# An encoder trunk on one core: the first norm's scale and shift made tile by tile, and one instruction order kept out of 24

## The chip, the cores and the metric

The kernel runs on one core of one Trainium2 chip. The core has a matrix engine (TensorE, PE in the profile), a vector engine (VectorE, DVE), a scalar engine (ScalarE, ACT), a general engine (GpSimd, POOL), and a sync engine (SyncE, SP) from whose queue this kernel issues its DMAs. Sixteen DMA engines move data between the memory of the chip and the core. The metric is the time of one execution on the device in microseconds, median of several runs; less is better.

## The reference, cut to what matters

One layer over 2048 tokens of 1024 features, all in float32: a norm whose scale and shift come from a conditioning vector, a combined projection, three kinds of recurrent heads, an output projection, a second such norm and a gated feed-forward block.

```python
cond = silu(c)                                   # (1, 1024)
mod = cond @ ada_w + ada_b                       # (1, 6 * 1024)
sh_m, sc_m, g_m, sh_f, sc_f, g_f = split(mod, 6)
h = rms_norm(x, norm_mix) * (1.0 + sc_m) + sh_m  # the first norm and its modulation
proj = h @ w_in
...                                              # retention, RWKV-7, mLSTM on parts of proj
x = x + g_m * (mixed @ w_out)
h = rms_norm(x, norm_ffn) * (1.0 + sc_f) + sh_f
gate, up = split(h @ ffn_w_in, 2)
x = x + g_f * ((silu(gate) * up) @ ffn_w_out)
return rms_norm(x, final_norm)
```

The change touches how `sh_m` (1024 shifts, 1024 x 1024 weights) and `sc_m` (as many) are made, and when.

## The kernel before

Everything is held transposed: features on the 128 partitions, tokens along the free dimension. The 1024 features are 8 tiles of 128 (`KT = 8`), the 2048 tokens are 4 blocks of 512 (`T`). A projection column (128 outputs of `w_in`, a "slot" of `winA`) is 8 weight tiles of 128x128, one for each feature tile, and each is multiplied three times (`mm3`: high weight with high data, high with low, low with high part) so that float32 precision comes out of fp32r passes; that makes 24 matmuls of 128x512 a column and block. Before use a weight half (256 KB) is loaded into a buffer `wraw`, cast to its high part by ScalarE (`split_in`) and subtracted to its low part by VectorE or GpSimd.

**Order.** The program text does not issue anything directly. Each call (`tt`, `stt`, `act`, `mmi`, `dma` ...) is recorded by `Sched.wrap` with its engine, an estimate of its cost and the tiles that it reads and writes. `Sched.emit` then lays all of them out with a list scheduler: each engine takes, among the operations that are ready by the estimates, the one of the best priority of its stage (`PRIO`) and then of the lowest place in the program. A result counts as ready for another engine after a latency from a table plus `margin`, 0.16 us. Dependences go by whole tiles. The operations are issued in that order, so each engine's order is fixed at build time, and every instruction has the one line L343 in the profile, that of the issuing loop. Buffers of a kind (`tag`) are given out in the order of first use.

**Lanes.** `dense()` does the projections and the feed-forward block (stages A, U, G, F), lanes P, C and M the recurrent heads, `ada_late()` the later modulation vectors, and `warm()` records 18 dummy matmuls at the lowest priority, which fill holes at the start.

**The head of `dense()`**, which the change rewrites, deals with block 0:

- Four tiles of `ada0` (the 1024 columns of `ada_w` that make `sh_m`, 128 rows each, 512 KB) are loaded into buffers `big`, then the 8 tiles of x (`xload`, 256 KB each), then the conditioning vector to all partitions (`cond_load`, tile `cond`, 512 KB), then the other four `ada0` tiles.
- `ada_shift`: TensorE multiplies the column `csil[:, k]` with each `ada0` tile, in two halves of 512 outputs, summed over all 8 tiles in PSUM (tile `dn`). ScalarE copies the two rows out, 8 tiny matmuls turn them into columns and one VectorE operation adds the bias: `shift_m`, all 8 tiles' shifts at once.
- `Sumsq` squares the x tiles (ScalarE), adds them up (VectorE, tile `acc`), and `fin` turns the sum into 1/rms, spread over all partitions (`bc`, in the tile `acc`): transposes on TensorE, a reduction on VectorE, a power on GpSimd (`rrs`), matmuls and a copy.
- `ada(1, m, ...)` makes the scale of feature tile m on VectorE: it loads 512 KB of `adaT`, the transposed `ada_w`, into one of 4 buffers `g` (tile `adaw`), multiplies with `cond` and sums along the row (accumulated output) into `gain_m[m]`.
- The first projection loop runs over feature tiles m = 0 to 7: the scale is finished, x is multiplied by `bc`, ScalarE and VectorE make the high and low part `h` (buffers `big`), and the 3 matmuls of each column loaded so far follow; five columns in all (two in `w`, three in spare tiles AR/ATA, ATB/BKt, UV/mt). So the loop holds 5 x 8 x 3 = 120 matmuls of 128x512.

There are 9 buffers `big`: `cond`, and the 8 `ada0` tiles, which give way to the 8 tiles `h`. The shifts and scales serve the later blocks too (`gsh_m`).

Of the kernel before, what the change touches and what calls it, by code (L numbers as in the profile page):

```python
# [50 lines left out]
for _n, _w in CONST_SPEC:  # L51
# [7 lines left out]
CFG = dict(w=4, raw=4, big=9, g=4, x=8, tmp=5, per=2, vd=1, nt=2, inv=1, xi=1, pr=1, x2=1, ld=2, wg=2, t1=4, gb=4, base=1, mt=2, mc=8,  # L59
           cv=1, mb=1, r1=4, dn=4, mx=2, ch=1, ml=1, bc=2, s2=1, hold=2.5, margin=0.16, warm=18, ahead=2, sm=1, a1=2, wm=0, wc=0.4, fa=True, ff=True, fh=True, nw=5, ws=2, fp=(0, 3, 6))  # L60
PRIO = dict(W=99, U=-20, A=-8, G=2, F=3, C=-7.5, P=-5, M=-4.9, S=-4)
# [3 lines left out]
class Sched:  # L65
# [9 lines left out]
    def __init__(self, prio, margin):  # L75
        self.ops = []
        self.stage = ("A", 0)
        self.prio = prio
        self.margin = margin
        self.flags = set()  # L80
        self.hist = {}
        self.bufs = {}
        self.psum = set()
        self.changes = 0

# [96 lines left out]
    def emit(self):  # L182
        import heapq

        n = len(self.ops)
# [22 lines left out]

        tag_of, uses, queue, free = {}, {}, {}, {}
        for tag, h in self.hist.items():  # L210
            h = sorted((x for x in h if x in touch), key=lambda x: touch[x][0])
            queue[tag] = h[::-1]
            free[tag] = [0.0] * self.bufs[tag]
            for x in h:
                tag_of[x] = tag
                uses[x] = len(set(touch[x]))
                left[touch[x][0]] += 1
        ready = [0.0] * n
        time = {e: 0.0 for e in self.ENG}
# [39 lines left out]
        while True:  # L259
# [56 lines left out]
            if e == "pe":  # L316
                m = op[2][e][2]
                if m != pe_mode:
                    end += 0.2 if op[2][e][0] > 0.1 and m == whole else 0.095
                    pe_mode = m  # L320
                    self.changes += 1
            chosen[j] = e
            time[e] = end
            order.append((t, j))
            for i in succ[j]:
                e2 = self.ops[i][0]
                r = end + self.LAT[e][e2]
                if e != e2:
                    r += self.margin
                met(i, r)  # L330
# [7 lines left out]
        assert len(order) == n, "a cycle through the buffers"  # L338
        self.end = max(time.values())
        order.sort()  # L340
        for t, j in order:
            op = self.ops[j]
            op[2][chosen[j]][1](*op[5], **op[6])  # L343


@with_exitstack
def trunk(ctx: ExitStack, tc: tile.TileContext, a: dict):
# [57 lines left out]
    def dps():  # L405
        return L.tile(pd, [P, 512], F32, "dn", K["dn"], nm("dn"))
# [10 lines left out]
    def tmp():  # L417
        return L.tile(tp, [P, 512], F32, "tmp", K["tmp"], nm("tmp"))
# [89 lines left out]
    gain_m = [cp.tile([P, 1], F32, name=f"gain_m{k}") for k in range(KT)]  # L508
    shift_m = cp.tile([P, KT], F32, name="shift_m")
    gbias = cp.tile([P, KT], F32, name="gbias")  # L510
# [3 lines left out]
    def gsh_m(k):  # L514
        return gain_m[k], shift_m[:, k:k + 1]
# [1265 lines left out]
def _prep(inp):  # L1781
# [30 lines left out]
    def put(name, v):  # L1812
# [47 lines left out]
```

## Time and profile before

| what | value |
|---|---|
| median of 3 runs | 2838.6 us (2829.53 to 2845.41) |
| the profiled execution | 2837.28 us |
| its span in the profile | 2835.5 us |
| mean granted TensorE clock | 0.994 of full |
| TensorE busy | 2763.7 us, 97% of the span |
| VectorE busy | 1927.6 us, 68% |

The profiled execution is 1.8 us longer than its span, and 1.3 us under the median. Times in the profile count from the start of the span. A matmul's busy time overlaps that of the next, so its rate is read from the starts of successive ones. "Idle before" names what an engine waited for last.

### The profile page before, as it was taken

To read this page: it belongs to the slowest core of one execution; us is meant where nothing else is said; L and a number is where in the kernel's file an instruction comes from. 1 tells how busy PE (TensorE), PEld (TensorE's weight loads), DVE (VectorE), ACT (ScalarE), POOL (GpSimd) and SP (SyncE) were. 2 spreads that over 40 slices of the span, in tenths; PEclk is the share of its full clock that TensorE was granted. 3 is DMA by queue.
4 is the path that set the end of the run, shared out by engine and by line. 5 is a ranking of instruction groups with operands and counts; after the bars stand their busy time and mean duration, and the time that the engine had idled before them with its cause. 6 is when DMAs were issued, how large, how long until landed. Compare 5 with 4: busy or idle time off the path is not lost.

```text
span 2835.5 us, 43320 instructions
## 1 busy us (share of the span) xinstructions
PE 2763.7 (97%) x14378; PEld 2263.1 (80%) x14378; DVE 1927.6 (68%) x5505; ACT 841.9 (30%) x1793; POOL 888.7 (31%) x1082
## 2 busy tenths in 40 slices
PE   8999999999999999999999999999999999999998
PEld 5877877887787787888778787787778888788887
DVE  6788789787787978764788877658778763422223
ACT  4445335434434433333322221122131211200002
POOL 2325645534536364431434132222223300000001
PEclk9999999999999999999999999999999999999999
DMA  8976556456655678888886556577765557775553
GB/s 321 318 229 196 158 170 195 144 163 230 203 154 157 226 237 262 280 281 306 263 279 195 185 184 199 183 246 241 237 196 171 181 194 241 258 248 192 194 193 137
DMA packets 349806, 613.04 MB, mean 216 GB/s; under 512 B 95528, under 2 KB 172944, under 8 KB 349584
## 3 DMA queue, kind: packets, MB, share of 16 engines
q1 hardware_dynamic: 349584, 610.29, 66.0%
q8 instruction: 114, 1.87, 0.3%
q14 instruction: 108, 0.88, 0.1%
HBM read 471.42 MB, written 138.73 MB: 215 GB/s over the span
## 4 chain that ended last, share of the span: by engine, by line
PE 74%; DVE 13%; DMA 7%; issue 2%; ACT 1%; POOL 1%; SPq 1%; POOLq 0%; DVEq 0%; ACTq 0%
PE dn L343 63%; PE mx L343 5%; PE ml L343 3%; PE ch L343 3%; DVE pr L343 2%; DVE tmp L343 2%; DMA tmp<-in_xT 1%; DVE mc L343 1%; DVE t L343 1%; DVE xi L343 1%; DMA w<-wsave 1%; DVE x L343 1%; SPq L343 1%; DMA adaw<-in_adaT 1%; DMA out<-x 1%
## 5 line engine op out<-in xcount | busy, mean ns | idle before, releaser
L343 PE MATMUL dn<-h,w 128*128 128x512 f32 x6648 | 1640.1, 398 | 13.0 <-DVE h L343 6.1
L343 PEld LDWEIGHTS dn<-h,w 128*128 128x128 f32 x6648 | 1223.1, 189 | 258.4 <-DVE h L343 10.7
L343 PE MATMUL dn<-g,w 128*128 128x512 f32 (+1 forms) x2112 | 506.8, 392 | 7.5 <-DMA w<-wsave 3.7
L343 PEld LDWEIGHTS dn<-g,w 128*128 128x128 f32 x2112 | 382.1, 188 | 84.6 <-issue 3.0
L343 POOL TENSOR_TENSOR w<-wraw,w 128x512 fp32r<-128x512 f32 (+1 forms) x243 | 315.0, 1298 | 395.1 <-ACT w L343 307.2
L343 ACT CAST w<-wraw 128x512 fp32r<-128x512 f32 (+1 forms) x414 | 246.1, 595 | 511.2 <-PE dn L343 357.5
L343 DVE TENSOR_TENSOR pr<-base,xi 128x20 f32<-128x20 f32 (+23 forms) x768 | 245.6, 320 | 26.4 <-POOL xi L343 12.4
L343 DVE SCALAR_TENSOR_TENSOR tmp<-tmp,dn 128x512 f32<-128x512 f32 x96 | 65.7, 685 | 250.5 <-PE dn L343 249.9
L343 DVE SCALAR_TENSOR_TENSOR x<-dn,mod,x 128x512 f32<-128x512 f32 x192 | 141.6, 747 | 118.9 <-PE dn L343 115.5
L343 PE MATMUL dn<-mT,w 128*128 128x512 f32 x768 | 187.6, 396 | 1.4 <-DMA w<-wsave 1.3
L343 DVE TENSOR_TENSOR w<-wraw,w 128x512 fp32r<-128x512 f32 (+1 forms) x171 | 114.8, 674 | 79.4 <-ACT w L343 74.9
L343 PEld LDWEIGHTS dn<-mT,w 128*128 128x128 f32 x768 | 141.3, 188 | 31.1 <-DMA w<-wsave 2.5
L343 POOL TENSOR_TENSOR rrs<-rst,mhalf 128x4 f32<-128x4 f32 (+1 forms) x13 | 15.6, 1203 | 465.2 <-DVE rst L343 443.7
L343 ACT ACTIVATE tmp<-dn 128x512 f32<-128x512 f32 x108 | 64.3, 596 | 313.1 <-PE dn L343 312.6
L343 DVE TENSOR_REDUCE xi<-pr 128x16 f32<-128x256 f32 (+30 forms) x768 | 146.3, 190 | 11.3
L343 ACT CAST g<-tmp 128x512 fp32r<-128x512 f32 x88 | 54.6, 620 | 309.3 <-DVE tmp L343 309.0
L343 PE MATMUL dn<-w,h 128*128 128x324 f32 x768 | 128.6, 319 | 2.3 <-DVE w L343 1.6
L343 PEld LDWEIGHTS dn<-w,h 128*128 128x128 f32 x768 | 116.1, 190 | 3.9 <-DVE w L343 1.8
L343 DVE SCALAR_TENSOR_TENSOR mc<-cv,pcol,mc 96x256 f32<-96x256 f32 x192 | 108.7, 566 | 11.6 <-ACT mc L343 9.8
L343 POOL TENSOR_SCALAR rSd<-rS,dfac 128x128 f32<-128x128 f32 x93 | 65.9, 709 | 147.3 <-DVE rS L343 111.6
L343 ACT COPY Y<-ch 64x128 f32<-64x128 f32 x93 | 24.1, 259 | 174.0 <-PE ch L343 172.5
L343 DVE SCALAR_TENSOR_TENSOR rS<-ch,dfac,rSd 64x64 f32<-64x64 f32 x186 | 52.4, 282 | 31.8 <-PE ch L343 27.5
(301 smaller groups left out, 3331.3 us busy)
## 6 DMA issues: line engine op xcount, KB each, us to landing
w<-wsave SPq DMA_DIRECT2D x440, 512.0 KB, 3.6
wsave<-w SPq DMA_DIRECT2D x148, 512.0 KB, 4.2
wraw<-in_winA SPq DMA_DIRECT2D x208, 256.0 KB, 3.1
wraw<-in_wfi SPq DMA_DIRECT2D x88, 256.0 KB, 3.6
adaw<-in_adaT SPq DMA_DIRECT2D x40, 512.0 KB, 5.9
tmp<-in_xT SPq DMA_DIRECT2D x72, 256.0 KB, 4.0
base<-nbuf SPq DMA_DIRECT2D x24, 512.0 KB, 5.6
wraw<-in_wfo SPq DMA_DIRECT2D x44, 256.0 KB, 5.3
```

The source lines that it names most:

```text
L343: op[2][chosen[j]][1](*op[5], **op[6])
```

## The change

The modulation of feature tile m becomes a step of its own, `modulation(m)`, made just ahead of that tile's turn in the loop; `ada_shift` goes away. For m = 1, 3, 5, 7 the 128 shifts come from TensorE (`shift_pe`): one 512 KB block of `ada0`, which the host lays out anew so that it holds all 1024 rows for the 128 columns of tile m, and 8 matmuls that use the 128x128 pieces as weights and one column of `csil` as data, into the PSUM buffer of lane C (`cps`); VectorE adds the bias out of PSUM. For m = 0, 2, 4, 6 they come from VectorE (`shift_dve`), as the scales do, from `adaT`. The shifts stand in two tiles, even and odd. The weights of the TensorE shifts use buffers `big`, together with `cond` and the 8 tiles `h`; those of VectorE the 4 buffers `g`. The squares of x come ahead of `cond` in the program.

`emit` now lays the whole program out 24 times, with margins of 0.160, 0.162, ... 0.206 us, and issues the order whose last engine ends first by the scheduler's own estimates. That concerns the order of all 43,000 instructions, not the head alone.

```diff
-CFG = dict(..., hold=2.5, margin=0.16, warm=18, ...)
+CFG = dict(..., hold=2.5, margin=0.16, layouts=24, mstep=0.002, warm=18, ...)
+PE_SHIFT = (1, 3, 5, 7)
...
+        best = None
+        for i in range(CFG["layouts"]):
+            r = self.layout(self.margin + CFG["mstep"] * i, succ, list(left), touch, tag_of, dict(total), firsts)
+            if best is None or r[0] < best[0]:
+                best = r
+        self.end, order, chosen = best
+        for t, j in order:
+            op = self.ops[j]
+            op[2][chosen[j]][1](*op[5], **op[6])
+
+    def layout(self, margin, succ, left, touch, tag_of, uses, firsts):
...
-    shift_m = cp.tile([P, KT], F32, name="shift_m")
+    shifts = [cp.tile([P, KT // 2], F32, name=f"shift_m{k}") for k in range(2)]
+    shift_m = [shifts[k % 2][:, k // 2:k // 2 + 1] for k in range(KT)]
...
-    def ada0_load(k):
-        w = L.tile(bp, [P, D], F32, "big", K["big"], nm("adaw"))
-        dma(w, a["ada0"][k * P:(k + 1) * P, :])
-        return w
-
-    def ada_shift(ws):
-
-        pss = [dps(), dps()]
-        for k, w in enumerate(ws):
-            yield [mmi(pss[i][0:1, :], csil[:, k:k + 1], w[:, i * 512:(i + 1) * 512], k == 0, k == KT - 1) for i in range(2)]
-        row = tmp(), tmp()
-        for r, ps in zip(row, pss):
-            acopy(r[0:1, :], ps[0:1, :])
-        pcol_ = dps()
-        yield [mmi(pcol_[:, k:k + 1], row[k // 4][0:1, (k % 4) * P:(k % 4 + 1) * P], ones[0:1, 0:1], True, True)
-               for k in range(KT)]
-        tt(shift_m, pcol_[:, 0:KT], pcs("ada_b", 0, KT), ALU.add)
+    def shift_pe(m):
+
+        w = L.tile(bp, [P, D], F32, "big", K["big"], nm("adaw"))
+        dma(w, a["ada0"][m])
+        ps = cps()
+        yield [mmi(ps[:, 0:1], w[:, k * P:(k + 1) * P], csil[:, k:k + 1], k == 0, k == KT - 1) for k in range(KT)]
+        tt(shift_m[m], ps[:, 0:1], pcs("ada_b", m), ALU.add)
+
+    def shift_dve(m):
+        ada(0, m, gp, "g", K["g"], shift_m[m])
+        tt(shift_m[m], shift_m[m], pcs("ada_b", m), ALU.add)
+
+    def gain_dve(m):
+        ada(1, m, gp, "g", K["g"], gain_m[m])
+        stt(gain_m[m], gain_m[m], gbias[:, m:m + 1], pcs("norm_mix", m), ALU.add, ALU.mult)
...
-        aw = [ada0_load(k) for k in range(4)]
         x0 = [xload(0, k) for k in range(KT)]
-        cond_load()
-        aw += [ada0_load(k) for k in range(4, KT)]
-        yield from ada_shift(aw)
         for k in range(KT):
             q.add(x0[k], True)
-
-        def ada_first(m):
-            ada(1, m, gp, "g", K["g"], gain_m[m])
-
-        for m in range(K["a1"]):
-            ada_first(m)
+        cond_load()
+
+        def modulation(m):
+            if m in PE_SHIFT:
+                yield from shift_pe(m)
+            else:
+                shift_dve(m)
+            gain_dve(m)
+
+        yield from modulation(0)
...
         for m in range(KT):
-            if m >= K["a1"]:
-                ada_first(m)
+            if m:
+                yield from modulation(m)
...
-            stt(g, g, gbias[:, m:m + 1], pcs("norm_mix", m), ALU.add, ALU.mult)
...
-"ada0": np.ascontiguousarray(f("ada_w")[0][:, 0:D]),
+"ada0": np.ascontiguousarray(f("ada_w")[0][:, 0:D].reshape(KT, P, KT, P).transpose(2, 1, 0, 3)).reshape(KT, P, D),
```

## Rows read from the trace of the kernel before

**Rows 1.** The page, part 1: busy us and share of each engine.

```profile
PE 2763.7 (97%) x14378; PEld 2263.1 (80%) x14378; DVE 1927.6 (68%) x5505; ACT 841.9 (30%) x1793; POOL 888.7 (31%) x1082
```

**Rows 2.** Windows: busy us (instructions) by engine, clock, DMA share, GB/s.

```profile
10.00:20.00 10.00, 7.02 (x34) 3.43 (x33) 3.92 (x6) 4.97 (x9) 0.41 (x1) 0.99 1.01 376
20.00:30.00 10.00, 10.00 (x29) 2.75 (x27) 5.31 (x11) 2.53 (x5) 2.04 (x2) 0.84 1.00 388
30.00:40.00 10.00, 4.82 (x22) 3.85 (x23) 9.94 (x14) 7.09 (x13) 5.29 (x3) 0.67 0.73 254
40.00:50.00 10.00, 10.00 (x37) 8.00 (x37) 8.83 (x17) 5.38 (x10) 1.03 (x1) 0.81 0.99 324
...
60.00:70.00 10.00, 10.00 (x46) 8.23 (x45) 6.57 (x14) 3.97 (x7) 3.62 (x3) 1.00 0.97 352
```

**Rows 3.** Timeline of 0 to 45 us: start, length, instruction, idle before.

```profile
6.61 7.03 PE L343 MATMUL dn<-adaw,csil 128*1 128x512 f32 x16 [0.54 <-DMA adaw<-in_ada]
...
18.18 0.63 ACT L343 ACTIVATE tmp<-cond 128x512 f32<-128x512 f32 x1 [2.72 <-DMA cond<-in_c]
...
24.71 0.66 PE L343 MATMUL dn<-const,acc 128*128 128x128 f32 x4
...
29.41 0.61 ACT L343 CAST w<-wraw 128x512 fp32r<-128x512 f32 x1
...
29.91 1.94 PE L343 MATMUL dn<-const,tmp 1*128 1x1 f32 x16
30.02 0.58 ACT L343 COPY acc<-dn 128x512 f32<-128x512 f32 x1
...
30.66 0.74 DVE L343 SCALAR_TENSOR_TENSOR x<-x,gain_m,acc 128x512 f32<-128x512 f32 x1
...
35.29 0.16 DVE L343 TENSOR_TENSOR shift_m<-dn,pcol 128x8 f32<-128x8 f32 x1
...
36.26 0.79 PE L343 MATMUL dn<-h,w 128*128 128x512 f32 x1 [4.41 <-ACT h L343]
...
37.82 2.50 PE L343 MATMUL dn<-h,w 128*128 128x512 f32 x5 [0.77 <-DVE h L343]
...
40.12 1.05 PE L343 MATMUL dn<-h,AR 128*128 128x512 f32 x2
```

**Rows 4.** Timeline of 45 to 90 us: the end of the first projection loop.

```profile
64.42 1.53 PE L343 MATMUL dn<-h,w 128*128 128x512 f32 x6
...
65.79 0.62 PE L343 MATMUL dn<-h,AR 128*128 128x512 f32 x2
...
67.84 18.98 PE L343 MATMUL dn<-h,w 128*128 128x512 f32 x83
```

**Rows 5.** Lines, VectorE, 30 to 68 us: count, busy us, mean ns, idle.

```profile
L343 DVE SCALAR_TENSOR_TENSOR adaw<-adaw,cond 128x1024 f32<-128x1024 f32 x10 | 13.1, 1320 | 0.0
L343 DVE TENSOR_TENSOR x<-x,acc 128x512 f32<-128x512 f32 x7 | 5.6, 797 | 0.0
L343 DVE TENSOR_TENSOR h<-x,h 128x512 fp32r<-128x512 f32 x7 | 5.3, 775 | 0.4 <-ACT x L343 0.4
L343 DVE SCALAR_TENSOR_TENSOR gain_m<-gain_m,gbias,pcol 128x1 f32<-128x1 f32 x7 | 4.2, 594 | 0.0
...
L343 DVE TENSOR_TENSOR ATA<-wraw,AR 128x512 fp32r<-128x512 f32 x2 | 1.4, 679 | 0.0
```

**Rows 6.** Windows of 2 us, 36:38 to 44:46: the clock, behind POOL.

```profile
36.00:38.00 2.00, 0.97 (x2) 0.47 (x3) 2.00 (x4) 1.97 (x4) 0.49 (x1) 0.50 0.72 272
...
42.00:44.00 2.00, 2.00 (x7) 1.57 (x6) 2.00 (x4) 0.00 (x0) 0.00 (x0) 0.57 1.02 341
44.00:46.00 2.00, 2.00 (x11) 1.61 (x10) 1.22 (x4) 1.61 (x3) 0.00 (x0) 1.00 0.95 318
```

**Rows 7.** Windows: 100 us to the end, columns as in the second group.

```profile
100.00:2835.00 2735.00, 2676.62 (x14023) 2201.87 (x14021) 1860.17 (x5386) 794.57 (x1713) 854.25 (x1043) 1.00 0.65 213
```

**Rows 8.** Waits of TensorE, 100 us to the end: total, times, longest.

```profile
PE dn L343 <- DMA w<-wsave: 7.2, 8, 1.8
```

More of the change, by code (lines that the diff above doesn't have):

```diff
@@ L59 @@
 CFG = dict(w=4, raw=4, big=9, g=4, x=8, tmp=5, per=2, vd=1, nt=2, inv=1, xi=1, pr=1, x2=1, ld=2, wg=2, t1=4, gb=4, base=1, mt=2, mc=8,
-           cv=1, mb=1, r1=4, dn=4, mx=2, ch=1, ml=1, bc=2, s2=1, hold=2.5, margin=0.16, warm=18, ahead=2, sm=1, a1=2, wm=0, wc=0.4, fa=True, ff=True, fh=True, nw=5, ws=2, fp=(0, 3, 6))
+           cv=1, mb=1, r1=4, dn=4, mx=2, ch=1, ml=1, bc=2, s2=1, hold=2.5, margin=0.16, layouts=24, mstep=0.002, warm=18, ahead=2, sm=1, a1=2, wm=0, wc=0.4, fa=True, ff=True, fh=True, nw=5, ws=2, fp=(0, 3, 6))
 PRIO = dict(W=99, U=-20, A=-8, G=2, F=3, C=-7.5, P=-5, M=-4.9, S=-4)
@@ L83, in __init__ @@
         self.psum = set()
-        self.changes = 0
     def tile(self, pool, shape, dt, tag, bufs, name):
@@ L182, in emit @@
     def emit(self):
-        import heapq
         n = len(self.ops)
@@ L207, in emit @@
                 touch.setdefault(x, []).append(j)
-        tag_of, uses, queue, free = {}, {}, {}, {}
+        tag_of, total, firsts = {}, {}, {}
         for tag, h in self.hist.items():
             h = sorted((x for x in h if x in touch), key=lambda x: touch[x][0])
-            queue[tag] = h[::-1]
-            free[tag] = [0.0] * self.bufs[tag]
+            firsts[tag] = h[::-1]
             for x in h:
                 tag_of[x] = tag
-                uses[x] = len(set(touch[x]))
+                total[x] = len(set(touch[x]))
                 left[touch[x][0]] += 1
+        best = None
[8 more added lines that the diff above has]
+    def layout(self, margin, succ, left, touch, tag_of, uses, firsts):
+        import heapq
+        n = len(self.ops)
+        queue = {tag: list(h) for tag, h in firsts.items()}
+        free = {tag: [0.0] * self.bufs[tag] for tag in firsts}
         ready = [0.0] * n
@@ L320, in emit @@
                     pe_mode = m
-                    self.changes += 1
             chosen[j] = e
@@ L328, in emit @@
                 if e != e2:
-                    r += self.margin
+                    r += margin
                 met(i, r)
@@ L338, in emit @@
         assert len(order) == n, "a cycle through the buffers"
-        self.end = max(time.values())
         order.sort()
-        for t, j in order:
-            op = self.ops[j]
-            op[2][chosen[j]][1](*op[5], **op[6])
+        return max(time.values()), order, chosen
 @with_exitstack
@@ L514, in gsh_m @@
     def gsh_m(k):
-        return gain_m[k], shift_m[:, k:k + 1]
-    def ada0_load(k):
+        return gain_m[k], shift_m[k]
+    def shift_pe(m):
         w = L.tile(bp, [P, D], F32, "big", K["big"], nm("adaw"))
-        dma(w, a["ada0"][k * P:(k + 1) * P, :])
-        return w
-    def ada_shift(ws):
-        pss = [dps(), dps()]
-        for k, w in enumerate(ws):
-            yield [mmi(pss[i][0:1, :], csil[:, k:k + 1], w[:, i * 512:(i + 1) * 512], k == 0, k == KT - 1) for i in range(2)]
-        row = tmp(), tmp()
-        for r, ps in zip(row, pss):
-            acopy(r[0:1, :], ps[0:1, :])
-        pcol_ = dps()
-        yield [mmi(pcol_[:, k:k + 1], row[k // 4][0:1, (k % 4) * P:(k % 4 + 1) * P], ones[0:1, 0:1], True, True)
-               for k in range(KT)]
-        tt(shift_m, pcol_[:, 0:KT], pcs("ada_b", 0, KT), ALU.add)
+        dma(w, a["ada0"][m])
[8 more added lines that the diff above has]
+        stt(gain_m[m], gain_m[m], gbias[:, m:m + 1], pcs("norm_mix", m), ALU.add, ALU.mult)
     def ada_late():
@@ L1835, in _prep @@
         "xT": np.ascontiguousarray(x.T), "c": f("c"),
-        "adaT": np.ascontiguousarray(f("ada_w")[0].T), "ada0": np.ascontiguousarray(f("ada_w")[0][:, 0:D]),
+        "adaT": np.ascontiguousarray(f("ada_w")[0].T), "ada0": np.ascontiguousarray(f("ada_w")[0][:, 0:D].reshape(KT, P, KT, P).transpose(2, 1, 0, 3)).reshape(KT, P, D),
         "ccol": np.ascontiguousarray(f("c").reshape(KT, P).T),
```

## The prediction

> **What bounds the kernel now.** I read the page's busy shares first: TensorE is busy 97% of the span [rows 1]. From 100 us to the end it stands idle 58.4 us of 2735, at full clock [rows 7], and the largest group of waits in that stretch is 7.2 us in eight pieces, the longest 1.8 us [rows 8]. So from 100 us on the kernel is a queue of TensorE work with small holes; what can be gained there in one place is small, and work that TensorE starts earlier should bring the end forward by about as much.
>
> Next the windows of the first 70 us [rows 2] and the timeline behind them [rows 3]. From 10 to 30 us the DMA engines are full (share 1.01 and 1.00, 376 and 388 GB/s), while TensorE does only the shifts, dummies and the norm's small matmuls. The first matmul of the projection loop starts at 36.26 us, after a wait of 4.41 us for ScalarE's `h`; `h` waited for the shifts, whose last step ran at 35.29. The loop's last matmul is issued just before 67.84, and 83 more follow without a hole [rows 4]. So 36.26 to 67.84 us, 31.6 us for 120 matmuls, is TensorE's own time. At full clock they follow one another at 0.228 us (six from 64.42 to 65.79 [rows 4]), 27.4 us; the other 4.2 us are mostly the lower clock: the granted clock is 0.50, the 1.2 GHz level, from 36 us and full from 44 [rows 6], and five matmuls from 37.82 take until 40.12 [rows 3], 0.46 us each, twice the full rate.
>
> The head is thus bound by loads, then by a chain through the shifts, and from 36 us by TensorE, with VectorE nearly as full (9.94 of 10 us in 30 to 40, 8.83 in 40 to 50 [rows 2]).
>
> **Part 1: the start of the loop.** Before the first `h`, eight 512 KB tiles of `ada0` have to land. Afterwards it is one 512 KB tile of `adaT`. At 382 GB/s, the mean of the two full windows [rows 2], such a tile takes 1.37 us.
>
> - `cond`: ScalarE got it at 18.18 us after waiting for that load [rows 3]. Four `ada0` loads go from ahead of it, 5.5 us: 12.7 us. The x tiles are ahead of it in the queue, the last in by about 11.3.
> - The norm: from the transposes of the squares' sum at 24.71 us to the end of the copy of `bc` at 30.60 is 5.9 us [rows 3]. The transposes stood behind the shifts' matmuls, which go. With a square and an add after the last x (1.4 us) they start near 12.7, and `bc` is ready at 18.6.
> - Tile 0's shift and scale: two `adaT` loads behind `cond` land at 15.4, two sums of 1.32 us [rows 5] and the small finishes end at 18.5. `cond`'s own four operations, which now stand behind the squares in the program, fit into the 2.7 us before that. The first weights (four 256 KB halves) follow, the first of them at 16.1, with a cast of 0.61 us [rows 3].
> - From `bc` to the first matmul the least is the x step, 0.74 us [rows 3], ScalarE's `h` and latencies, about 1.7 us. Before it was 5.7 us (30.60 to 36.26), because the shifts came late and VectorE's fixed order had sums in between.
>
> So the loop starts between 20.3 and 24.3 us; I take 21.0, near the lower end, because the shifts, which made the 5.7, are then there before `bc`. That is 15.3 us earlier.
>
> **Part 2: what the loop costs then.** Three engines have to be looked at.
>
> *TensorE.* The 120 matmuls stay, 27.4 us. Added are four shifts of 8 matmuls with 128x128 weights and one column, in two passes each: 16 instructions. The trace has no such shape; the nearest are the 16 tiny matmuls at 29.91, 1.94 us, and four transposes at 24.71, 0.66 us, which is 2.6 us for 16 [rows 3]. I take 1.94, since both have a single column of data and the weights set the pace: 7.8 us for four, of which one falls in a wait for tile 1, so 5.8 (bounds 0, all in waits, and 10.4). The shifts of before, 16 instructions in 7.03 us at 6.61 and as many later, cost nothing, since TensorE was waiting for loads. Undersupply: at 21 us two columns have weights; the other three columns' raw halves need the four `wraw` buffers free first, so TensorE has about 4 us of work for 6 us; 2 us lost (0 to 4). The lower clock: some stretch of it again, as the loop again starts after a pause; the same 4.2 us (0 to 8). Sum 27.4 + 5.8 + 2 + 4.2 = 39.4, loop over at 60.4.
>
> *VectorE.* It gets four more sums with their bias, 1.32 us each in these rows [rows 5], 5.3 us in all, and 4 bias additions out of PSUM. Over the loop: 12 sums at 1.32 (15.8), 16 steps of x and h at 0.8 (12.8), 8 finished scales at 0.59 (4.8), 8 bias additions at 0.16 (1.3) [rows 3], and 7 subtractions of weights at 0.68 (4.8) [rows 5], with three others left to GpSimd: 39.5 us. From 15.4 that ends at 54.9; the last tile's high part and 15 matmuls add 4.2: 59.1 us. So VectorE is 1.3 us from being the bound, and what the scheduler puts between (a later modulation sum is 1.32) decides. I take 60.8 us for the loop's end.
>
> *Loads.* From 12.7 us there are 16 tiles of 512 KB and ten halves of 256 KB, 21 x 1.37 = 28.8 us, done at 41.5. The fourth TensorE shift needs a `big` buffer, of which there are nine for `cond`, eight `h` and four such weights, so its load is issued only when an earlier shift is over; some 7 us of matmuls (30 at 0.228) lie between the two in TensorE's order, five times the 1.37 of the load. No price. A shift's matmuls wait for their load, and behind them in TensorE's fixed order stand the loop's matmuls of that tile and the next; tile 1's load is in at 15.4 + 2.7 + 1.4 = 19.5, ahead of the loop's start, and the last of all at 41.5, when TensorE is only half through.
>
> The loop's end goes from 67.84 to 60.8: 7.0 us earlier. Its bounds: 56 (start at 20.3, shifts in waits, VectorE's means a little shorter) and 74 (start at 24.3, all shifts at 2.6, 8 us of lower clock, 4 of undersupply), so 12 earlier to 6 later.
>
> *Behind it.* The 83 matmuls after the loop [rows 4] want weights 7 us sooner; a column takes 5.5 us and its load 1.4, so nothing is priced. VectorE's extra sums are then paid off: it is busy 6.57 of 10 us in 60 to 70 [rows 2].
>
> **Part 3: one order out of 24.** No row shows another order. From 100 us on there are 58.4 us of idle TensorE time [rows 7] that an order can shorten or lengthen; a quarter of it, 15 us either way, I take as bounds. The choice goes by the scheduler's estimates, and its estimates do speak of those holes, so I put a small gain on it, 2 us.
>
> **The sum.** 2835.5 - 7.0 - 2 = 2826.5 span, and 1.8 outside it: 2828.3 us against this execution's 2837.28, 0.3% less; I say 2828, 0.4% under the median of 2838.6. Half a per cent, 14.2 us, is about what a measurement of this kernel can tell from no change; faster begins at 2824.4, slower at 2852.8.
>
> **The rivals.**
>
> - *More than that.* The shifts fall into waits, the loop ends at 56, 12 us earlier, and the chosen order saves 5 us: 2835.5 - 12 - 5 + 1.8 = 2820. For it: the first 6 us of the loop have room for two shifts. Against it: VectorE's 59.1. Chance 0.27.
> - *Nothing.* The loop ends earlier, but the order returns it: 7 us in holes, 12% of 58.4, is enough; 2837. Then the loop would be shorter and the idle time after 100 us longer. It is also what comes out when `bc` or the fixed order holds the start at 24.3 and all shifts stand on TensorE. Chance 0.16.
> - *Slower by the clock.* In the trace TensorE gets 1.2 GHz after its pause of 32 to 36 us and keeps it for 8 us although the loop is running [rows 6]. A loop fed one tile at a time by loads and sums, with TensorE working in bursts, could stay there: 120 matmuls at 0.456 are 54.7 us, the shifts at double price 11.6, undersupply 2, so the loop ends at 89, 21.5 us later than before, and the time is 2857. Some 17 matmuls ran slowly before; about 100 more must do so before the time passes 2852.8, nearly the whole loop. Against it: at the lower clock TensorE would be the one that others wait for and so be busy throughout, and it was busy throughout when the clock rose at 44 us. Chance 0.04. The Trainium skill, "TensorE: Matmul & The Clock Gate", section "Loop structure matters more than you think", speaks for this rival: it sets a loop whose matmuls wait for a load in each turn, and which runs cold for it, against one whose matmuls follow back to back. By that rule the time is 2857; the trace agrees with it so far that the clock stands at 0.50 at 36 us after the pause.
> - *Slower by the order.* The new order makes 24 us more holes, 40% of the 58.4. Chance 0.05.
>
> **How the numbers follow.** The forecast's own case has 0.48, with 2821 to 2836 as its own range; 0.05 of it lies under 2824.4. So faster is 0.27 + 0.05 = 0.32, slower 0.04 + 0.05 = 0.09, same 0.59. The range 2814 to 2841 leaves out the two slower cases (0.09), the low tail of the first rival (0.05) and the high one of the second (0.04).
>
> **What would show it.** Right: no loads of `ada0` ahead of x, `cond` on ScalarE near 13 us, the first `h,w` matmul at 20 to 24, the 83-matmul run starting at 58 to 64, four groups of 16 tiny TensorE instructions of 2 us each, two or three of them between loop matmuls, VectorE near full from 18 to 55, idle time after 100 us within 50 to 70 us. Wrong: a loop that starts early but ends near 68 (part 2's terms too small), a clock of 0.50 through most of it, or an idle sum after 100 us that has moved by more than the head (part 3).

## The result, and the profile after

The median is 2824.65 us (2819.1 to 2828.2) against 2838.6 before. The ratio is 0.9943, with a 95% interval of 0.9931 to 0.9955: 0.57% faster, 0.49% by the medians alone. The forecast was 2828 us, 0.4%. So the time lies in the range, 3.4 us under the forecast, and on the bound between "no change" (0.59) and "faster" (0.32): the median is 0.25 us short of the 2824.4 that the prediction set for it, the ratio just past its half per cent. The profiled execution took 2823.16 us, its span 2821.4 us, 14.1 us less than before. All instructions now have the line L224.

First the windows, with the columns of [rows 2] and [rows 7]: busy us (instructions) of PE, PEld, DVE, ACT and POOL, then clock, DMA share and GB/s.

```profile
10.00:20.00 10.00, 3.19 (x12) 2.50 (x12) 9.00 (x14) 6.54 (x11) 4.34 (x4) 0.67 1.03 389
20.00:30.00 10.00, 7.56 (x25) 6.29 (x26) 9.80 (x15) 4.58 (x8) 3.54 (x3) 0.50 1.02 381
30.00:40.00 10.00, 9.83 (x59) 8.38 (x58) 10.00 (x24) 4.56 (x7) 0.00 (x0) 0.97 0.99 346
40.00:50.00 10.00, 10.00 (x47) 8.31 (x46) 10.00 (x18) 6.15 (x10) 4.25 (x3) 1.00 1.00 360
50.00:60.00 10.00, 10.00 (x51) 8.44 (x50) 7.59 (x14) 3.25 (x6) 0.00 (x0) 1.00 0.99 329
...
100.00:2821.00 2721.00, 2667.19 (x13990) 2195.36 (x13988) 1854.74 (x5382) 793.99 (x1708) 837.23 (x1023) 1.00 0.66 213
```

VectorE is nearly full from 10 to 50 us (9.00, 9.80, 10.00 and 10.00 of 10 us) and no longer in 50 to 60 (7.59). TensorE is busy 9.83 of 10 us in 30 to 40, where it had 4.82 [rows 2], and 10.00 from 40 to 60. From 100 us on it is idle 53.8 us instead of 58.4 [rows 7], and busy 2667.19 us instead of 2676.62.

The timeline of the head after: start, length, instruction, idle before.

```profile
13.60 1.15 ACT L224 ACTIVATE tmp<-cond 128x512 f32<-128x512 f32 x2 [0.97 <-DMA cond<-in_c]
...
16.54 1.23 DVE L224 SCALAR_TENSOR_TENSOR adaw<-adaw,cond 128x1024 f32<-128x1024 f32 x1
...
17.57 5.98 POOL L224 TENSOR_TENSOR w<-wraw,w 128x512 fp32r<-128x512 f32 x4 [0.19 <-DMA wraw<-in_winA]
...
17.69 2.29 DVE L224 SCALAR_TENSOR_TENSOR adaw<-adaw,cond 128x1024 f32<-128x1024 f32 x1
...
19.55 0.58 ACT L224 COPY acc<-dn 128x512 f32<-128x512 f32 x1
...
19.91 1.21 DVE L224 TENSOR_TENSOR shift_m<-shift_m,pcol 128x1 f32<-128x1 f32 x1
...
20.20 3.57 PE L224 MATMUL ch<-csil,adaw 128*128 128x1 f32 x16 [0.69 <-DMA adaw<-in_ada]
21.04 1.30 DVE L224 SCALAR_TENSOR_TENSOR gain_m<-gain_m,gbias,pcol 128x1 f32<-128x1 f32 x1
...
22.45 1.64 DVE L224 SCALAR_TENSOR_TENSOR x<-x,gain_m,acc 128x512 f32<-128x512 f32 x1
24.02 0.15 DVE L224 TENSOR_TENSOR shift_m<-ch,pcol 128x1 f32<-128x1 f32 x1
...
24.91 0.80 PE L224 MATMUL dn<-h,w 128*128 128x512 f32 x1 [1.14 <-ACT h L224]
...
30.95 0.15 DVE L224 TENSOR_TENSOR shift_m<-shift_m,pcol 128x1 f32<-128x1 f32 x1
...
35.80 0.43 SPq L224 DMA_DIRECT2D adaw<-in_ada  x1
...
37.41 1.92 PE L224 MATMUL ch<-csil,adaw 128*128 128x1 f32 x16 [0.17 <-DMA adaw<-in_ada]
...
61.95 15.92 PE L224 MATMUL dn<-h,w 128*128 128x512 f32 x69
```

The first matmul of the loop starts at 24.91 us, 11.35 us earlier than the 36.26 of [rows 3], and the unbroken run behind the loop's last matmul starts at 61.95 instead of 67.84 [rows 4]: 5.9 us earlier. Three VectorE rows, at 19.91, 21.04 and 22.45, are long for what they do: operations on one column take 1.21 and 1.30 us, and the x step, 0.74 us before [rows 3], takes 1.64. All begin beside the four GpSimd subtractions at 17.57 to 23.55. A bias addition of the same kind at 30.95, with GpSimd idle, takes 0.15 us. Such lengths are not new: the kernel before has a finished scale of 1.23 us and a sum of 2.28 beside three GpSimd subtractions, and the 594 ns and 1320 ns of [rows 5] are means over short and long ones. Timeline of the kernel before:

```profile
31.20 5.29 POOL L343 TENSOR_TENSOR w<-wraw,w 128x512 fp32r<-128x512 f32 x3 [2.89 <-ACT w L343]
31.33 1.23 DVE L343 SCALAR_TENSOR_TENSOR gain_m<-gain_m,gbias,pcol 128x1 f32<-128x1 f32 x1
...
33.08 2.28 DVE L343 SCALAR_TENSOR_TENSOR adaw<-adaw,cond 128x1024 f32<-128x1024 f32 x1
```

From the loop's end to the end of the span it is 2759.5 us, against 2767.7 before: 8.2 us less. Where that comes from is looked for in the first matmul of each block's output projection (tile `mT`):

| | loop end | block 0 | block 1 | block 2 | block 3 | span's end |
|---|---|---|---|---|---|---|
| before | 67.84 | 680.4 | 1352.6 | 1872.5 | 2390.6 | 2835.5 |
| after | 61.95 | 671.1 | 1345.1 | 1861.0 | 2375.6 | 2821.4 |
| earlier by | 5.9 | 9.3 | 7.5 | 11.5 | 15.0 | 14.1 |

So 5.9 us were there when the loop ended, and the rest came unevenly over some 2300 us. The rows of the windows from 100 us on split the 14.1 otherwise: 9.4 us are work that TensorE no longer had before it at 100 us (2676.62 less 2667.19), 4.6 are idle time that it had less of afterwards. TensorE's largest group of waits from 100 us on is 6.0 us in nine pieces, where it was 7.2 in eight [rows 8]. No single wait explains it.

```profile
PE dn L224 <- DMA w<-wsave: 6.0, 9, 1.2
```

### The profile page after: what moved, and what is told of

Its sections match the earlier page's. It is cut to its first block, busy times and chain, and to the rows that moved or that the text cites. A ratio compares the mean times of both kernels' runs of the same rounds, so it can differ in the third digit from the quotient of the medians.

```text
span 2821.4 us, 43359 instructions
## 1 busy us (share of the span) xinstructions
PE 2752.8 (98%) x14394; PEld 2267.0 (80%) x14394; DVE 1938.2 (69%) x5538; ACT 843.4 (30%) x1791; POOL 873.7 (31%) x1064
## 3 DMA queue, kind: packets, MB, share of 16 engines
q1 hardware_dynamic: 349584, 610.29, 66.3%
## 4 chain that ended last, share of the span: by engine, by line
PE 74%; DVE 12%; DMA 8%; issue 2%; POOL 1%; ACT 1%; SPq 1%; POOLq 0%; DVEq 0%; ACTq 0%
PE dn L224 63%; PE mx L224 4%; PE ml L224 4%; PE ch L224 3%; DVE pr L224 2%; DVE tmp L224 2%; DMA out<-x 1%; DMA w<-wsave 1%; DVE xi L224 1%; DVE mc L224 1%; DMA tmp<-in_xT 1%; SPq L224 1%; DVE mrow L224 1%; DVE h L224 1%; DVE x L224 1%
## 5 line engine op out<-in xcount | busy, mean ns | idle before, releaser
L224 PE MATMUL dn<-h,w 128*128 128x512 f32 x6648 | 1632.1, 397 | 7.1 <-DVE h L224 4.5
L224 PEld LDWEIGHTS dn<-h,w 128*128 128x128 f32 x6648 | 1221.0, 189 | 252.8 <-DVE h L224 8.3
L224 PE MATMUL dn<-g,w 128*128 128x512 f32 (+1 forms) x2112 | 507.3, 391 | 4.6 <-DMA w<-wsave 2.8
L224 PEld LDWEIGHTS dn<-g,w 128*128 128x128 f32 x2112 | 381.4, 188 | 81.9 <-DMA w<-wsave 2.1
L224 POOL TENSOR_TENSOR w<-wraw,w 128x512 fp32r<-128x512 f32 (+1 forms) x227 | 298.8, 1318 | 393.4 <-ACT w L224 311.3
L224 ACT CAST w<-wraw 128x512 fp32r<-128x512 f32 (+1 forms) x414 | 246.3, 596 | 518.6 <-PE dn L224 343.1
L224 DVE TENSOR_TENSOR pr<-base,xi 128x20 f32<-128x20 f32 (+23 forms) x768 | 240.7, 313 | 17.6 <-POOL base L224 2.1
L224 DVE SCALAR_TENSOR_TENSOR tmp<-tmp,dn 128x512 f32<-128x512 f32 x96 | 65.6, 684 | 253.9 <-PE dn L224 253.0
L224 DVE SCALAR_TENSOR_TENSOR x<-dn,mod,x 128x512 f32<-128x512 f32 x192 | 142.3, 749 | 120.0 <-PE dn L224 118.8
L224 PE MATMUL dn<-mT,w 128*128 128x512 f32 x768 | 192.3, 399 | 4.5 <-DMA w<-wsave 2.2
L224 DVE TENSOR_TENSOR w<-wraw,w 128x512 fp32r<-128x512 f32 (+1 forms) x187 | 129.5, 695 | 78.6 <-ACT w L224 72.3
L224 PEld LDWEIGHTS dn<-mT,w 128*128 128x128 f32 x768 | 141.7, 190 | 33.9 <-DMA w<-wsave 3.5
L224 ACT ACTIVATE tmp<-dn 128x512 f32<-128x512 f32 x108 | 64.4, 596 | 337.2 <-PE dn L224 334.3
L224 POOL TENSOR_TENSOR rrs<-rst,mhalf 128x4 f32<-128x4 f32 (+1 forms) x13 | 15.0, 1153 | 461.9 <-DVE rst L224 442.4
L224 DVE TENSOR_REDUCE xi<-pr 128x16 f32<-128x256 f32 (+30 forms) x768 | 147.1, 192 | 12.7
L224 ACT CAST g<-tmp 128x512 fp32r<-128x512 f32 x88 | 54.6, 620 | 333.9 <-DVE tmp L224 333.9
L224 PE MATMUL dn<-w,h 128*128 128x324 f32 x768 | 127.8, 316 | 0.6 <-ACT tmp L224 0.6
L224 POOL TENSOR_SCALAR rSd<-rS,dfac 128x128 f32<-128x128 f32 x93 | 63.8, 686 | 171.1 <-DVE rS L224 139.6
L224 PEld LDWEIGHTS dn<-w,h 128*128 128x128 f32 x768 | 114.7, 188 | 2.0 <-ACT tmp L224 0.8
L224 DVE SCALAR_TENSOR_TENSOR mc<-cv,pcol,mc 96x256 f32<-96x256 f32 x192 | 105.8, 551 | 9.2 <-ACT mc L224 7.9
L224 DVE SCALAR_TENSOR_TENSOR rS<-ch,dfac,rSd 64x64 f32<-64x64 f32 x186 | 52.4, 282 | 33.4 <-PE ch L224 31.0
L224 ACT COPY Y<-ch 64x128 f32<-64x128 f32 x93 | 24.1, 259 | 162.5 <-PE ch L224 158.9
```

## The experiments

Three theories were set against one another. **A**: the order decides; a new head changes the order of all that follows, and the scheduler's own estimate of the end (its *plan*, known without a chip) foresees in which orders the kernel is fast. **B**: the head decides; the time follows the loop's end, and the choice among 24 adds little. **C**, formed later from the runs: with a good order under each, the new head is worth about the 7 us of the prediction's part 2, and the choice of an order about as much.

The plan of the kernel before ends at 2790.5 us. The changed one chose the margin 0.166, and its text has two plans there, 2791.0 and 2787.3: `layout` goes through Python sets of tile names, whose order may change from one build to the next, and with it the order of the instructions. The expectations reckon with 2791.0, but the order that ran is the other. That of 2791.0 gives GpSimd 239 of the subtractions `w<-wraw,w`, that of 2787.3 gives it 227, and the page of the profile has 227:

```profile
L224 POOL TENSOR_TENSOR w<-wraw,w 128x512 fp32r<-128x512 f32 (+1 forms) x227 | 298.8, 1318 | 393.4 <-ACT w L224 311.3
```

So by the plan the two kernels lie 3.2 us apart, and on the chip 14. Below, the *surplus* is the measured median less the plan: 48.1 for before, 37.4 for after (33.7 by the plan of 2791.0).

### One part of the change without the other

**The new head in the old order's margin.**

```diff
-layouts=24, mstep=0.002
+layouts=1, mstep=0.002
```

> The new head, laid out once with the margin of before, 0.160 us. Theory A (the choice of the order decides, through two waits that the scheduler foresees): in this order the weights of tile 7's TensorE shift get their buffer some 12 us later, since tile 5's shift runs late; the plan ends the first projection loop 10 us later than in the chosen order (68.6 against 58.7) and all of it 21 us later (2811.6 against 2791.0). So the loop ends near 71 us on the chip, not 62, the output projection of block 0 starts some 30 us later, and the time is about 2845 us, slower than before the change. Theory B (the head gives 6 us whatever the order, orders differ by chance): loop end near 62 us, time 2826 to 2836 us.

Measured: 2854.08 us, ratio 1.0057 (1.0040 to 1.0073), slower than before. The loop starts at 25.5 us and ends at 75.9, eight us after that of before. The timeline of this run:

```profile
30.86 0.43 SPq L224 DMA_DIRECT2D adaw<-in_ada  x1
...
47.12 0.95 PE L224 MATMUL ch<-csil,adaw 128*128 128x1 f32 x8
...
51.46 0.95 PE L224 MATMUL ch<-csil,adaw 128*128 128x1 f32 x8
...
52.44 0.33 SPq L224 DMA_DIRECT2D adaw<-in_ada  x1
...
56.35 1.41 PE L224 MATMUL ch<-csil,adaw 128*128 128x1 f32 x6 [3.94 <-DMA adaw<-in_ada]
```

Tile 5's shift stands late in TensorE's order (47.12 and 51.46; in the changed kernel it is done by 39.3). Only when it is over does its `big` buffer come free, and so tile 7's weights are asked for at 52.44 instead of 35.80, and TensorE, with the loop's matmuls behind that shift, waits 3.94 us for them. The granted clock is 0.75 in that stretch. Later the mLSTM lane comes late, and TensorE has holes before block 0's output projection; that this follows from the late loop is not shown, as the run with margin 0.168 below has the late lane without the late loop. Windows of this run:

```profile
50.00:60.00 10.00, 6.06 (x28) 5.23 (x27) 8.37 (x15) 4.19 (x6) 3.27 (x2) 0.75 0.96 360
...
680.00:700.00 20.00, 12.56 (x59) 9.76 (x59) 16.45 (x46) 10.91 (x26) 9.65 (x10) 0.66 0.67 225
```

and the same stretch of the changed kernel, already in that projection:

```profile
680.00:700.00 20.00, 17.93 (x82) 13.49 (x83) 13.88 (x32) 11.57 (x28) 6.93 (x7) 0.91 0.83 279
```

The row of tile `mT` in the two (count, mean ns least/median/most, from when to when): 

```profile
L224 PE MATMUL dn<-mT,w x192: 387/389/628, 704.2 to 759.9; 128*128 128x512 f32 x192
```

```profile
L224 PE MATMUL dn<-mT,w x192: 387/389/641, 671.1 to 738.3; 128*128 128x512 f32 x192
```

The first is this run: its projection begins 33 us later.

**The same without the fourth TensorE shift**, so that no shift waits for a `big` buffer.

```diff
-PE_SHIFT = (1, 3, 5, 7)  layouts=24
+PE_SHIFT = (1, 3, 5)     layouts=1
```

> As the first of these runs (margin 0.160, one order), but tile 7's shift is made on VectorE, so that no TensorE shift has to wait for a buffer to come free. Theory A: the loop ends near 64 us (plan 61.5), 7 us earlier than with four TensorE shifts in one order, and the time is about 2834 us (plan 2800.8). Theory B: the buffer plays no part; the loop ends where that of the first run does, give or take 1 us.

Measured: 2842.22 us, 1.0018 (1.0008 to 1.0028). The loop ends at 64.6, 11.4 us earlier than with four, and the time falls by 11.9, which leaves it 0.18% over that of before (2834 was expected). That agrees with the buffer as what delayed the loop; but the edit also takes one shift's work off TensorE and draws a new order, so the 11.9 us are not the buffer's alone.

**The old head with the choice among 24.** The kernel before with the new `emit` and `layout`; it chooses the margin 0.172, plan 2785.3.

> The head of before with the choice among 24 orders alone; the scheduler keeps margin 0.172. Theory A: the estimates tell good orders from bad ones, and here the order of before was already a good one (plan 2790.5, the chosen one 2785.3): about 5 us faster than before, 2833 us. Theory B: the choice is worth nothing or anything, 2830 to 2847 us.

Measured: 2832.46 us, 0.9981 (0.9972 to 0.9991), with the loop from 34.3 to 64.9. The choice alone gives 0.2%.

**The old head in an order whose plan is bad** (2816.5).

```diff
-margin=0.16
+margin=0.18
```

> The head of before, one order with margin 0.180, which the scheduler puts 26 us behind that of 0.160 (2816.5 against 2790.5), because the mLSTM lane of block 0 ends 35 us later and the output projection of block 0 waits for it. Theory A: TensorE has a hole or low use ahead of that projection, it starts some 25 us later than before (680.7 us), and the time is about 2860 us. Theory B: the estimates are too coarse for that, 2830 to 2847 us.

Measured: 2858.99 us, 1.0071 (1.0056 to 1.0086), though the loop ends at 66.5, a little earlier than before. Block 0's output projection begins at 704.2, as in the first experiment. The windows and the timeline of this run show TensorE at the lower level of its clock (0.50) and waiting for the mLSTM lane:

```profile
680.00:700.00 20.00, 13.94 (x62) 11.44 (x62) 12.95 (x38) 8.91 (x23) 4.79 (x5) 0.50 0.31 92
```

```profile
675.36 2.04 PE L343 MATMUL ml<-qp,mt 128*128 128x256 f32 x4 [3.73 <-POOL mt L343]
```

With these four, B falls: an order 2 hundredths of a microsecond of margin away costs 20 us with nothing changed in the head. A had the third and fourth time within 1 us. The first two it put 9 and 8 us too low, so that the second, which it had faster than before, is not; and the first loop's end it put 5 us too early.

### How far the plan can be trusted

**Margins under those of the 24**, whose plans are the best that the new head has here (2785.3 and 2779.2):

```diff
-margin=0.16, layouts=24
+margin=0.123, layouts=1
```

> The changed kernel with one order, margin 0.123, which by the scheduler's estimates ends at 2785.3, 5.7 us ahead of the chosen one. Theory A (the estimates, with 39 to 43 us added that they lack in the first four runs, give the chip's time within some 6 us): 2820 to 2830 us, loop end near 61 us. Theory B (below some 10 us the estimates tell nothing, and a smaller margin makes more waits): slower than 2830.

```diff
-PE_SHIFT = (1, 3, 5, 7)  margin=0.16, layouts=24
+PE_SHIFT = (1, 3)        margin=0.095, layouts=1
```

> Only tiles 1 and 3 have their shifts made by TensorE, one order with margin 0.095, the best of several hundred orders by the estimates: 2779.2, 11.8 us ahead of the chosen one of the change, loop end 58.6 in the plan as there. Theory A: 2813 to 2823 us, faster than the changed kernel (2824.65); no load of shift weights waits for a buffer. Theory B: a margin this small lets engines be planned ahead of their data; more waits on TensorE, 2825 us or more.

Measured: 2856.84 us, 1.0053 (1.0035 to 1.0072), and 2848.14, 1.0041 (1.0028 to 1.0054). Both miss what the plan promised; the surplus is 71.5 and 69. Windows of the first:

```profile
100.00:600.00 500.00, 478.27 (x2630) 400.52 (x2629) 402.32 (x1193) 215.41 (x471) 233.47 (x264) 0.99 0.61 192
600.00:2400.00 1800.00, 1757.97 (x9326) 1430.84 (x9325) 1320.32 (x3984) 514.43 (x1129) 604.50 (x753) 0.99 0.66 216
```

and of the changed kernel:

```profile
100.00:600.00 500.00, 485.54 (x2728) 408.54 (x2727) 413.55 (x1250) 220.01 (x475) 222.04 (x257) 1.00 0.62 192
600.00:2400.00 1800.00, 1772.19 (x9370) 1446.68 (x9369) 1314.86 (x3935) 518.48 (x1134) 604.97 (x755) 1.00 0.68 221
```

TensorE is idle 21.7 and 42.0 us in these stretches instead of 14.5 and 27.8. That fits an order which counts on results 0.04 us sooner and then waits for them a little everywhere. So A holds only among margins from 0.16 on, where the surplus was 37 to 49 in twelve kernels.

### What bounds the loop

**All shifts on VectorE** (24 orders, 0.170 chosen):

```diff
-PE_SHIFT = (1, 3, 5, 7)
+PE_SHIFT = ()
```

> All eight shifts on VectorE, best of 24 orders (margin 0.170, plan 2792.2, loop end 63.3 in the plan). It tests the division between TensorE and VectorE. By the prediction's sums VectorE then has four more sums of 1.3 us and TensorE loses its 6 to 8 us of shifts, so VectorE sets the loop's end, near 66 us on the chip; the time by theory A is about 2833 us. If the division were worth nothing, the loop would end near 62 us and the time be 2825.

Measured: 2837.17 us, 0.9998 (0.9988 to 1.0008). Windows of this run:

```profile
30.00:40.00 10.00, 7.79 (x23) 4.66 (x22) 9.30 (x16) 5.41 (x9) 2.85 (x2) 0.82 0.96 314
40.00:50.00 10.00, 7.66 (x31) 5.66 (x32) 9.67 (x18) 4.49 (x7) 4.12 (x4) 1.00 0.97 323
50.00:60.00 10.00, 8.92 (x37) 6.72 (x38) 10.00 (x20) 4.15 (x6) 0.91 (x1) 1.00 0.92 322
```

VectorE stays full and TensorE has only 7.7 to 8.9 of 10 us of work: VectorE is the bound. The loop's last matmul ends near 65.3, 3.6 us later than in the changed kernel (its last one begins at 61.44 and ends near 61.7), and the run behind it starts only at 67.63, 5.7 us later. The division of the shifts between the engines thus counts in the loop. The time is 12.5 us longer, 4 more than the 2833 that A gave; what the loop does not account for is put down to the order, which is not shown.

**More dummy matmuls at the start**, to keep the clock up (24 orders, 0.164 chosen):

```diff
-warm=18
+warm=60
```

> 60 dummy matmuls instead of 18, 24 orders (margin 0.164, plan 2796.6, loop end 62.8 in the plan). In the changed kernel TensorE has the lower clock from about 13 to 31 us and the loop ends 3.0 us later than planned. If the lower clock is the cause of that delay, it is gone with the fillers: clock near full from 13 to 31 us, the first shift near 1.9 us instead of 3.6, loop end at 63 to 64 us. If loads or VectorE set the pace there, the clock rises and the loop still ends 3 us late, near 66 us. Time by theory A about 2837 us.

Measured: 2845.75 us, 1.0031 (1.0020 to 1.0042). Windows and timeline of this run:

```profile
10.00:20.00 10.00, 5.82 (x48) 5.25 (x47) 8.26 (x13) 5.71 (x10) 4.24 (x4) 1.00 1.02 393
20.00:30.00 10.00, 9.46 (x58) 8.73 (x59) 9.88 (x16) 4.54 (x8) 3.60 (x3) 0.83 0.96 360
...
40.00:50.00 10.00, 9.42 (x47) 7.72 (x45) 8.73 (x19) 4.99 (x8) 2.94 (x3) 1.00 0.98 312
50.00:60.00 10.00, 9.46 (x53) 8.25 (x54) 6.94 (x14) 2.30 (x4) 0.00 (x0) 1.00 0.96 332
```

```profile
20.32 1.97 PE L224 MATMUL ch<-csil,adaw 128*128 128x1 f32 x16 [0.58 <-DMA adaw<-in_ada]
...
25.14 0.66 PE L224 MATMUL dn<-h,w 128*128 128x512 f32 x1
```

The clock is 1.00 and 0.83 where the changed kernel has 0.67 and 0.50, and the first shift takes 1.97 us instead of 3.57. Yet the loop starts at 25.1 as before, and ends at 66.3. The plan of this order ends it at 62.8 and that of the changed kernel at 58.7, so each is 3 us or so behind its plan: the clock bought nothing that can be seen, though the two orders differ. What sets the loop's pace here is not shown: VectorE is no longer full after 40 us (8.73 and 6.94 of 10). The time is 9 us over A's 2837.

### Does an early loop alone bring it?

**The neighbouring margin**, the only other one of the 24 whose plan ends the loop early (58.8; in the other 22 it is near 68.6):

```diff
-margin=0.16, layouts=24
+margin=0.168, layouts=1
```

> The changed kernel with one order, margin 0.168, the neighbour of the chosen 0.166 and the only other of the 24 whose plan ends the first loop early (58.8); but its plan lets the mLSTM lane of block 0 end 29 us later (657 against 628) and ends at 2799.4. Theory A (an early loop alone is worth little: what the later lanes make of it decides): loop end near 62 us as in the changed kernel, the output projection of block 0 some 15 to 25 us later than there (671), time near 2843 us. Theory B (the early loop brings the gain): 2822 to 2830 us.

Measured: 2841.44 us, 1.0015 (1.0002 to 1.0027). The loop ends at 62.2, 0.3 us after that of the changed kernel, but the row of `mT` of this run begins 23 us later:

```profile
L224 PE MATMUL dn<-mT,w x192: 387/389/628, 694.0 to 747.3; 128*128 128x512 f32 x192
```

An early loop brings no gain where the mLSTM lane comes late.

**Two more divisions in orders with good plans** (2786.2 and 2786.4):

```diff
-PE_SHIFT = (1, 3, 5, 7)  margin=0.16, layouts=24
+PE_SHIFT = (1, 3)        margin=0.1715, layouts=1
```

> Shifts of tiles 1 and 3 on TensorE, the rest on VectorE, one order with margin 0.1715, the best of 110 between 0.160 and 0.215 by the estimates (2786.2; loop end 60.9 in the plan). For margins from 0.16 to 0.18 the chip has so far been 41 to 49 us above the plan, but 34 for the changed kernel. Theory A: 2786.2 + 44 = 2830 us, within 5, loop end near 64 us: no better than the changed kernel, whose own order is some 8 us better than its plan says. If the changed kernel's smaller surplus belongs to the new head and not to its order, 2820 us.

```diff
-PE_SHIFT = (1, 3, 5, 7)  margin=0.16, layouts=24
+PE_SHIFT = (1, 3, 5)     margin=0.1835, layouts=1
```

> Shifts of tiles 1, 3 and 5 on TensorE, one order with margin 0.1835, again the best of 110 by the estimates (2786.4; loop end 61.6 in the plan). As for the run before: 2830 us within 5 by the usual surplus of 44, loop end near 65 us; 2820 us if the smaller surplus belongs to the new head.

Measured: 2825.33 us, 0.9951 (0.9936 to 0.9966), and 2824.49, 0.9953 (0.9934 to 0.9972): level with the changed kernel, at the lower edge of "2830 within 5" and well over 2820. The second text has two plans as well; its trace is that of the plan of 2785.4 (236 of the subtractions on GpSimd, not 228), so the surplus is 39.1 in both. In the second the loop ends only at 66.7, 1.1 us before that of the kernel before, and yet the time is that of the changed kernel. So an early end of the loop is neither enough (margin 0.168) nor needed.

**The old head in its second good order** (plan 2785.5):

```diff
-margin=0.16
+margin=0.178
```

> The head of before with one order, margin 0.178, which the scheduler puts level with its best of 110 for that head (2785.5 against 2785.3 at 0.172). Three new-head orders with plans of 2786 to 2791 took 2824.5 to 2825.3 us on the chip, two old-head orders with plans of 2785 and 2790 took 2832.5 and 2838.2. Theory C (the new head is worth some 7 to 10 us when both heads have a good order): 2830 to 2835 us. Theory D (the head is worth nothing once the order is good, the old head's two were unlucky): 2822 to 2827 us.

Measured: 2831.17 us, 0.9973 (0.9959 to 0.9987).

That makes three good orders of the new head (0.9943, 0.9951, 0.9953) and two of the old (0.9973, 0.9981). The means are 0.9949 and 0.9977: the new head is worth 0.28%, 8 us, and a good order on the old head 0.23%, 6.5 us, together 0.51% of the 0.57% that was measured. That is C, resting on five orders, all picked by their plans, and the price depends on how they are picked: the best of 24 for both heads gives 0.9943 against 0.9981, 10.8 us, and the margin 0.160 for both makes the new head 0.57% slower. The order with all shifts on VectorE, the best of its 24 with a plan of 2792.2, is not among them and gains nothing. No kernel run here is clearly faster than the changed one.

## Why the prediction came out as it did

The time is in the range, and the loop starts and ends earlier through shifts made tile by tile, as predicted. Two terms were off in opposite directions, the loop's gain too high by 1.1 us and the order's too low by more. That the sum still lay in the range is in part luck: no row foresaw the order, and at the margin of before the same head takes 2854. The premise that work which TensorE starts earlier brings the end forward by about as much did not hold order by order: loop ends at 61.95 and 62.2 went with 2824.65 and 2841.44 us, one at 66.7 with 2824.49.

- **Start of the loop: 24.91, said 21.0 (20.3 to 24.3).** `cond` came at 13.60 (12.7 said) and `bc` at 20.13 (18.6). Then "the shifts, which made the 5.7, are then there before `bc`" failed. Tile 0's shift and scale were priced from the sums of 1.32 us and "small finishes", from 15.4 us on. The first sum began at 16.54, behind VectorE's work on `cond` and the norm; then, beside GpSimd's subtractions, the second sum took 2.29, the two finishes 1.21 and 1.30, and the x step 1.64. So they ended at 22.3 instead of 18.5, and from `bc` to the first matmul it was 4.8 us, not 1.7. The mis-sized term is VectorE's durations, taken from rows without looking at which of them ran beside GpSimd. The scheduler's estimates share a part of this: its function `ports` counts only inputs of more than one element, so it plans the one-column finishes as if GpSimd did not touch them.
- **The loop: 37.0 us, said 39.4.** A shift takes 1.92 us at full clock (1.94 said); the three in the loop, read from the starts of successive instructions, 5.1 (5.8 said). The lower clock costs about 1.8 (4.2 said): it ends near 30.5, 5.6 us into the loop, with nine matmuls at twice the time. (The 4.2 held some waiting as well: in the kernel before 14 matmuls ran slowly, not 17, which is 2.9 us.) Holes between the matmuls come to about 2.8 (2 said), more than half of it before 27 us. VectorE was full to 50 us as the prediction had it, but from 31 us on TensorE hardly waited: there the loop was its own time. The loop's end came 5.9 us earlier, 7.0 said.
- **"No price" for the fourth shift's buffer.** Right in the order that was chosen (issued at 35.80, and tile 7's shift, begun at 46.13, does not wait) and wrong as a rule: the argument "some 7 us of matmuls lie between the two in TensorE's order" counted a program order that the scheduler does not keep. In the old margin the wait is 3.94 us, and making that shift on VectorE there, with the new order that this brings, gave 11.9 us back.
- **The choice among 24: 2 us, measured 6.5 on the old head.** This is the larger part of the miss to the low side, and its price for the new head is greater: without the choice (2854.08) the change would have made the kernel 0.57% slower. The "slower by the order" case, given 0.05, is what the new head does at the old margin. The prediction treated head and choice as terms to be added; with this head the choice decides the sign.
- **The rivals.** "Nothing" fell: the idle time after 100 us went down by 4.6 us. "More" had the order right and the head wrong. "Slower by the clock" fell: it needed nearly all 120 matmuls at the lower level, nine had it, and the clock rose at some 30.5 us while the loop was being fed tile by tile. The rule cited for it, of the Trainium skill's "TensorE: Matmul & The Clock Gate", section "Loop structure matters more than you think", is about a loop with a long wait at each turn, and this loop has none: the longest wait of TensorE in it is 1.1 us. In the run with more dummies a higher clock in the first part did not end the loop sooner, in another order.

**Left open.** Why good orders of the new head lie 37 to 39 us above their plan and those of the old head 46 to 48. The loop's end does not tell it, but the work that TensorE still has before it at 100 us points the same way as the times, in one profiled execution of each:

| kernel | loop end | TensorE busy after 100 us | idle after 100 us | span |
|---|---|---|---|---|
| before | 67.8 | 2676.6 | 58.4 | 2835.5 |
| old head, margin 0.172 | 64.9 | 2672.5 | 55.5 | 2828.0 |
| old head, margin 0.178 | 66.0 | 2669.6 | 56.4 | 2826.1 |
| changed kernel | 61.95 | 2667.2 | 53.8 | 2821.4 |
| two shifts on TensorE, 0.1715 | 61.5 | 2666.0 | 57.0 | 2823.4 |
| three shifts on TensorE, 0.1835 | 66.7 | 2667.7 | 51.3 | 2819.8 |

With a good order the new head leaves 2 to 6.5 us less work than the old one at 100 us; the idle time behind it varies by as much, in many small holes and no one place. One more `big` buffer, which would do away with the fourth shift's wait in every order, has no room in SBUF.

## What to carry to other kernels

When a list scheduler orders the whole program, an edit to its first 60 us redraws the other 2760; judge the edit by the better of several orders on both sides, or what is measured is the luck of one order (here 29 us between margins of 0.160 and 0.166, almost four times the edit's own worth). A plan's end tells good orders of one head from bad ones, is some 9 us off between two heads, and misleads where it counts on results sooner than they come. When the scheduler goes through sets, fix their order, or one text gives several programs. A mean over a group hides two lengths of one operation: ask of each what ran beside it. A buffer that a new step takes from a shared pool has a price in the order that is issued, not in the one that is written.

## What the runs showed of the hardware

**VectorE is held up by GpSimd, small operations most of all in proportion.** In the changed kernel's timeline a bias addition takes 1.21 us at 19.91 and 0.15 at 30.95; the four GpSimd subtractions beside the first take 5.98 us, 1.5 each, so the small operation looks as if it waited one of them out. It also goes the other way: two GpSimd operations of one shape, the first of which starts in the middle of a VectorE sum, and two finished scales, 0.21 us each where GpSimd is idle, that take 1.94 behind that sum. Timeline of the changed kernel:

```profile
46.56 1.21 DVE L224 SCALAR_TENSOR_TENSOR adaw<-adaw,cond 128x1024 f32<-128x1024 f32 x1
...
46.66 1.99 POOL L224 TENSOR_TENSOR lwa<-tmp,lwa 128x384 fp32r<-128x384 f32 x1 [4.87 <-ACT lwa L224]
...
47.71 1.94 DVE L224 SCALAR_TENSOR_TENSOR gain_m<-gain_m,gbias,pcol 128x1 f32<-128x1 f32 x2
...
48.61 1.02 POOL L224 TENSOR_TENSOR lg<-tmp,lg 128x384 fp32r<-128x384 f32 x1
```

GpSimd's 1.99 is roughly 1.02 and the rest of the sum; VectorE's two scales end at 49.65, with the second GpSimd operation at 49.63. Operations with an input out of PSUM show no such lengthening. In the kernel before, the bias addition at 35.29 took 0.16 us [rows 3] with GpSimd at work from 31.20 to 36.49. And over the whole trace of the changed kernel two groups of one operation and shape differ in where they read (least/median/most in ns; `dn` lies in PSUM, both full inputs of the other in SBUF):

```profile
L224 DVE SCALAR_TENSOR_TENSOR x<-dn,mod,x x192: 653/751/754, 686.7 to 2742.3; 128x512 f32<-128x512 f32 x192
L224 DVE SCALAR_TENSOR_TENSOR h<-tmp,shift_m,h x24: 714/742/1772, 217.0 to 746.6; 128x512 fp32r<-128x512 f32 x24
```

Of the 192, 78 overlap GpSimd work by their times, and none is lengthened. Of the 24, 15 do, up to 1772 ns, and the nine others stay within 750. The Trainium skill, "SBUF — State Buffer", section "SBUF: two separate sides", describes this as a lock: a VectorE operation with two inputs in SBUF and a GpSimd operation that reads SBUF share a pair of ports, and the one that starts first keeps it for its whole length. The rows agree in both directions, the operations out of PSUM included; no run here took GpSimd's work away to test it.

**A shift on TensorE goes by the clock.** Sixteen instructions with 128x128 weights and one column took 3.57 us where the granted clock was 0.50 (20 to 30 us) and 1.92 at full clock.
